# Seven outer products split a second time, with the inner instances of two products interleaved

## The chip, the cores and the metric

The kernel runs on one core of a Trainium2 chip. The metric is device time in microseconds (us), from runs of the whole program. The engines are TensorE (PE, matrix products), VectorE (DVE), ScalarE (ACT), GpSimd (POOL) and SyncE (SP). In this kernel POOL and SP mostly issue transfers (DMAs). Each engine works through its own list of instructions in order; a waiting instruction holds up all that stand behind it on that engine.

## What is computed

A soft mixture of experts: every token goes through all 8 experts, and the results are added with the softmax of the router's logits as weights.

```python
batch, seq, hidden, n_experts, expert_hidden = 16, 512, 512, 8, 2048
probs = softmax(router_logits, axis=-1)          # (16, 512, 8)
for e in range(n_experts):
    expert_out = np.matmul(x, expert_weights[e])  # (16, 512, 512) x (512, 2048)
    output += probs[:, :, e:e+1] * expert_out
```

Scaling the rows of x by the probabilities first turns this into one product of matrices, Z (8192 tokens by 8 x 512) times W (8 x 512 by 2048), with the sum over the experts inside it. The kernel works in 16-bit floats and adds up in 32 bits.

## The kernel before

The big product is cut in two along each of its three dimensions: rows into even and odd blocks of 256 tokens (one even and one odd block are a row pair, 16 of them), experts into two groups of four (2048 of the inner dimension), and columns into two halves of 1024. A scheme of the Strassen-Winograd kind turns the 8 block products into 7, which the code numbers 1 to 7 and which are called outer products here. Their left operands are sums and differences of blocks of Z, their right operands of blocks of W. One outer product of one row pair has 256 rows, 2048 inner and 1024 columns. Computed directly it takes 64 matmuls of 128x128 by 128x512.

Products 1, 5, 2 and 4 are computed by `sub_product`, one after the other over all row pairs. It splits each product once more by the same scheme, with the two row pairs of a step as the two halves of its rows: 7 inner instances, each of two row blocks of 8 matmuls (`K8 = 8`), where the direct form needs 8. Results of products 1, 2 and 5 go to memory of their own (`kept`) and those of 4 to the output. Behind them, a loop over the 16 row pairs (`for q in range(NI)`) computes products 6 and 7 directly (`plain`, 64 matmuls each), and product 3 by an inner split within the row pair (`prod`, 7 instances of 8 matmuls; for q = 0 directly). It reads back what was kept and writes the output, part of it by DMAs that add to what stands there. The first two row pairs of product 1 are computed directly at the very start, while the weights are still arriving.

Left operands are made by DVE: `mul` or `times` multiplies transposed x with probabilities (128 partitions by 2048 elements, 16 bits), and differences of such tiles follow. Right operands of the inner split are made by `inner_sums`, whose four steps (5, 6, 4, 7) each are one DVE operation over 128 by 4096. Weight tiles have 15 places (`wpool`), left tiles 10 (`zpool`), x and probability tiles 8 (`xpool`), and half tiles (128 rows by 512 columns in 32 bits, `half`) 15. PE adds up in 8 banks of PSUM of that size.

The order of the work on each engine comes from two sources. Where `pinned` holds (the start, and the loop over row pairs), DVE and ACT instructions keep the order in which the code writes them (`keep_in_program_order` in `dve`); in `sub_product` a scheduler at compile time chooses. DMAs of POOL and SP and the matmuls are placed by that scheduler throughout, with a few pinned by `behind`.

The lines that matter in the profile: line 142 is `mm`, every matmul; line 122 is `tt`, every two-operand DVE operation, to be told apart by tile names (z left tiles, w weight tiles, h half tiles, ps banks) and shapes; line 136 is POOL's loads, line 133 SP's DMAs, line 594 POOL's stores to the output, line 404 ACT's copies out of PSUM in `sub_product`, line 669 those in the loop.

Of the kernel before, what the change touches and what calls it, by code (L numbers as in the profile page):

```python
# [20 lines left out]

# [11 lines left out]
def kernel(  # L33
# [7 lines left out]
    nc = tc.nc  # L41
# [24 lines left out]
    zpool = ctx.enter_context(tc.tile_pool(name="zpool", bufs=10))  # L66
    xpool = ctx.enter_context(tc.tile_pool(name="xpool", bufs=8))
    hpool = ctx.enter_context(tc.tile_pool(name="hpool", bufs=1))
# [5 lines left out]
    used = {i: -1 for i in range(15)}  # L74
    places = {}
    turn = count()

    def share(**sizes):

        order = sorted(used, key=used.get)  # L80
        for use, n in sizes.items():
            places[use], order = [order[:n], 0], order[n:]

    def h_tile(shape, dtype, use="any"):
        mine, i = places[use]
        places[use][1] = (i + 1) % len(mine)
        used[mine[i]] = next(turn)
        return hpool.tile(shape, dtype, name="h", tag=f"h{mine[i]}")

    share(any=15)  # L90


# [3 lines left out]


# [10 lines left out]

    pinned = [True]

    def note(i):
        last[i.ins.engine] = i.ins

    def dve(i):
        note(i)
        if pinned[0]:
            tc.keep_in_program_order(i)
# [17 lines left out]
    def pool(o, i):  # L135
        note(nc.gpsimd.dma_start(out=o, in_=i))  # L136
# [4 lines left out]
    def mm(ps, z, w, start, stop):  # L141
        nc.tensor.matmul(ps, z, w, start=start, stop=stop, skip_group_check=True)  # L142


# [5 lines left out]

    def cast_w(q, kn, e, t, parts=1):
        k, n = kn
        for c in range(0, C, C // parts):
            pool(t[:, ds(e * C + c, C // parts), :],
                 expert_weights[(q // 10 - 1) * HE + 2 * k + e, ds(c * P, C * P // parts),
                                ds((q % 10 - 1) * NH + n * NB, NB)].rearrange("(c p) n -> p c n", p=P))

    def load(what, kn, gate=True):
        t = new_w()
        if gate:  # L160
            dve(nc.vector.memset(t.rearrange("p (e c) n -> p e c n", e=2)[:, :, 0, 0:2], 0.0))  # L161
        if (what, kn) in stored:
            pool(t, stored[what, kn])
        else:
            for e in range(2):
                cast_w(what, kn, e, t)
        return t

    def store(what, kn, t):
        stored[what, kn] = d = dram.tile([P, K8, NB], f16, name=f"wd{what}_{kn[0]}{kn[1]}")  # L170
        sp(d, t)

    def inner_sums(b, t3=None):

        t3 = t3 or b[0, 1]
        w = {1: b[0, 0], 2: b[1, 0], 3: b[1, 1], 7: t3}

        def step(p, x, y):
            if p not in w:
                w[p] = new_w()  # L180
            tt(w[p], x, y, SUB)
        return w, [lambda: step(5, b[0, 1], b[0, 0]), lambda: step(6, b[1, 1], w[5]),
                   lambda: step(4, w[6], b[1, 0]), lambda: step(7, b[1, 1], b[0, 1])]

    def inner_weights(b):
        w, sums = inner_sums(b)
        sums[0]()
        yield
        sums[1]()
        sums[2]()  # L190
        yield
        sums[3]()
        return w


    def softmax(lg, J, pf=None):
# [7 lines left out]
        if pf is None:  # L204
            pf = h_tile([P, E, J], f32)
# [5 lines left out]
    P2, P1, PQ = 0, HE, 2 * HE  # L211

# [25 lines left out]
    with behind():  # L238
        for kn in BLOCKS[:3]:
            for e in range(2):  # L240
                cast_w(11, kn, e, b11[kn], 2 if kn == (0, 0) and e == 0 else 1)
    cast_x(4)
    cast_x(6)
    for e in range(2):
        cast_w(11, BLOCKS[3], e, b11[BLOCKS[3]])

    def early_p(t):
        return softmax(lg0[t], 4, cpool.tile([P, HE, 4], f16, name=f"ph0_{t}"))
# [13 lines left out]

# [12 lines left out]

# [18 lines left out]

# [13 lines left out]
    def softmax_of_all():  # L308
        pf = softmax(lg_all, J)
        ph = h_tile([P, 3 * HE, J], f16)  # L310
        nc.scalar.copy(ph[:, 0:HE], pf[:, HE:E])
        nc.scalar.copy(ph[:, HE:2 * HE], pf[:, 0:HE])
        tt(ph[:, 2 * HE:], pf[:, 0:HE], pf[:, HE:E], ADD)
        for r in range(R):
            sp(p_dram[:, :, ds(r * J, J)], ph[ds(r * NHQ, NHQ)])


    x_dram = {}
    x_new = []

    def load_x(h):
        xT = xpool.tile([P, C, HQ], f16, name="xT", tag="x")
        if h in x_dram:
            sp(xT, x_dram[h])
        else:
            xs = h_tile([P, HQ // P, H], f16, "xs")
            pool(xs, x_f[ds(h * HQ, HQ), :].rearrange("(j p) h -> p j h", p=P))
            for j in range(HQ // P):
                note(nc.sync.dma_start_transpose(out=xT[:, :, ds(j * P, P)], in_=xs[:, j, :]))
            x_new.append((h, xT))  # L330
        return xT

    def store_x():
        while x_new:
            h, xT = x_new.pop()
            x_dram[h] = dram.tile([P, C, HQ], f16, name=f"x_{h}")
            sp(x_dram[h], xT)

    def load_p(h, first):
        pT = xpool.tile([P, HE, HQ], f16, name="pT", tag="x")  # L340
        sp(pT, p_dram[h, ds(first, HE), :].partition_broadcast(P))
        return pT

    def mul(xT, pT, e0, ne, t0, nt):
        z = zpool.tile([P, ne, C, nt], f16, name="z", tag="z")
        tt(z, xT[:, :, ds(t0, nt)].unsqueeze(1).to_broadcast([P, ne, C, nt]),
           pT[:, ds(e0, ne), ds(t0, nt)].unsqueeze(2).to_broadcast([P, ne, C, nt]), MUL)
        return z.rearrange("p e c t -> p (e c) t")


    kept = {r: [dram.tile([2, HQ, NB], f32, name=f"kept{r}_{i}") for i in range(NI)] for r in (1, 2, 5)}

    def half(use="any"):
        return h_tile([P, NB], f32, use)

    def out_rows(i, odd, u, cols, n):
        return out_f[ds((2 * i + odd) * HQ + u * P, P), ds(cols * NH + n * NB, NB)]

    def to_kept(r, i, u, n, t):
        if r == 4:  # L360
            sp(out_rows(i, 1, u, 0, n), t)
        else:
            sp(kept[r][i][n, ds(u * P, P), :], t)

    def from_kept(r, i, u, n, use):
        t = half(use)
        sp(t, kept[r][i][n, ds(u * P, P), :])
        return t

    def sub_product(r, odd, first, w, prep, start=0, xp=None, rest=()):  # L370

        for d in range(start, NI // 2):
            hs = [4 * d + odd, 4 * d + 2 + odd]
            xp = xp or [(load_x(h), load_p(h, first)) for h in hs]
            a11, a12 = (mul(*xp[0], e0, 2, 0, HQ) for e0 in (0, 2))
            a21, a22 = (mul(*xp[1], e0, 2, 0, HQ) for e0 in (0, 2))
            xp = None

            def new(a, b, op):
                z = zpool.tile([P, K8, HQ], f16, name="z", tag="z")  # L380
                tt(z, a, b, op)
                return z
            s1 = new(a21, a22, ADD)
            s2 = new(s1, a11, SUB)
            s4 = new(a12, s2, SUB)
            tt(a21, a11, a21, SUB)
            for make in rest:
                make()
            rest = ()
            z = {1: a11, 2: a12, 3: s4, 4: a22, 5: s1, 6: s2, 7: a21}  # L390

            for u in range(HQ // P):
                banks = {}

                def prod(p, b, start=True):
                    if start:
                        banks[b] = bank()
                    for k in range(K8):
                        mm(banks[b], z[p][:, k, ds(u * P, P)], w[p][:, k, :], start and k == 0, k == K8 - 1)
                    return banks[b]  # L400

                def keep(ps):
                    t = half("r")
                    nc.scalar.copy(t, ps)  # L404
                    return t

                def put(t, n, a, b, op):
                    o = half("o")
                    tt(o, a, b, op)
                    to_kept(r, 2 * d + t, u, n, o)  # L410

                r1 = keep(prod(1, "x"))
                put(0, 0, prod(2, "b"), r1, ADD)
                r5 = keep(prod(5, "q"))
                r2 = keep(prod(6, "x", False))
                put(0, 1, prod(3, "q", False), r2, ADD)
                prod(7, "x", False)
                r3 = keep(banks["x"])
                put(1, 1, banks["x"], r5, ADD)
                put(1, 0, r3, prod(4, "d"), SUB)  # L420
            with behind():
                store_x()
                next(prep, None)
# [349 lines left out]
```

## Time and profile before

| what | value |
|---|---|
| time, median of 3 runs | 1433.58 us (1433.33 to 1433.64) |
| span of the profiled execution, first to last instruction | 1431.8 us |
| other time given for that execution | none; the span is 1.8 us under the median |
| PE busy | 1424.9 us, 100% |
| DVE busy | 1031.8 us, 72% |
| ACT busy | 271.0 us, 19% |
| POOL busy | 220.0 us, 15% |
| matmuls at line 142 with left tiles | 6560 |
| moved by DMA | 318.92 MB, 223 GB/s on average |

How to read it. The shares are busy time over the span. A busy PE may still be slower than its peak, because matmuls overlap: each has 379 ns from its start to its end, but the next one starts long before that. The chain that ended last goes back from the last instruction to what released it, step by step, and so says which engine sets the end. A line of a group of instructions has the code line, the engine, the operation, the tiles written and read, the shapes, the count, and then the total busy time, the mean of one in nanoseconds, and the idle time ahead of these instructions with what ended it. A line of the view in order of time has the start, the duration, the engine, the line, the operation and the count of instructions merged into it; what stands in brackets is the idle time before and its releaser. Instructions of one engine can overlap a little, so the distance of two starts can be less than a duration.

### The profile page before, as it was taken

The page shows a single profiled execution, that of the slowest core. Times are in us where ns is not written, and L with a number is a line of the kernel's source. Part 1 is how long each engine was busy: PE and PEld are TensorE (multiplying, and loading weights), DVE is VectorE, ACT ScalarE, POOL GpSimd, SP SyncE. Part 2 cuts the span into 40 slices and gives each one's busy share as a digit, 9 for nine tenths or more (in the row PEclk, how much of TensorE's full clock was granted, in tenths as well). Part 3 has the DMA queues.
Part 4 walks back from the last instruction along what each step waited for, and adds up shares of the span by engine and source line. Part 5 has one row for each costly group of instructions (what it writes and reads, how often), then busy time and mean ns, then how long its engine had stood idle before and what let it go on. Part 6 is the DMA issues. An engine that isn't in the chain of part 4 may idle for free.

```text
span 1431.8 us, 18014 instructions
## 1 busy us (share of the span) xinstructions
PE 1424.9 (100%) x6654; PEld 648.0 (45%) x6654; DVE 1031.8 (72%) x1177; ACT 271.0 (19%) x472; POOL 220.0 (15%) x344
## 2 busy tenths in 40 slices
PE   9999999999999999999999999999999999999998
PEld 4444444444444444444444444444444444444444
DVE  6967585657686867766767687777777877877773
ACT  3211111111111111111111211111111111111111
POOL 3111100110001000001000222222222222222220
PEclk9999999999999999999999999999999999999999
DMA  9899967899649994367875977787877777778774
GB/s 196 182 252 267 273 160 192 183 256 262 204 148 305 350 333 155 132 186 220 219 250 179 311 218 232 235 239 230 229 231 223 206 216 215 225 234 241 215 199 103
DMA packets 192041, 318.92 MB, mean 223 GB/s; under 512 B 51664, under 2 KB 80592, under 8 KB 187344
## 3 DMA queue, kind: packets, MB, share of 16 engines
q1 hardware_dynamic: 135328, 202.92, 45.2%
q0 software_dynamic: 56624, 114.84, 34.1%
q8 instruction: 52, 0.85, 0.2%
q14 instruction: 37, 0.30, 0.1%
HBM read 180.13 MB, written 159.58 MB: 237 GB/s over the span
## 4 chain that ended last, share of the span: by engine, by line
PE 98%; DMA 1%; POOL 0%; DVE 0%; issue 0%; POOLq 0%
PE ps L142 98%; DMA w<-in_expert_weights_dram 1%; POOL w L136 0%; DVE z L122 0%; DVE h L122 0%; POOL ident L235 0%; POOLq L235 0%; POOLq L757 0%
## 5 line engine op out<-in xcount | busy, mean ns | idle before, releaser
L142 PE MATMUL ps<-w,z 128*128 128x512 f16 x6560 | 1415.2, 379 | 1.2 <-DMA w<-in_expert_weights_dram 0.9
L142 PEld LDWEIGHTS <-z 128*128 128x128 f16 x6560 | 641.6, 98 | 773.6 <-DVE z L122 1.1
L122 DVE TENSOR_TENSOR h<-ps,h 128x512 f32<-128x512 f32 x389 | 268.0, 689 | 328.5 <-PE ps L142 94.4
L122 DVE TENSOR_TENSOR z<-xT,pT 128x2048 f16<-128x2048 f16 x252 | 304.2, 1218 | 32.6 <-PE ps L142 31.2
L122 DVE TENSOR_TENSOR z<-z 128x2048 f16<-128x2048 f16 x280 | 303.6, 1108 | 7.3
L404 ACT COPY h<-ps 128x512 f32<-128x512 f32 x248 | 145.3, 586 | 602.0 <-PE ps L142 596.0
L594 POOL DMA_DIRECT2D out_dram<-h x244 | 154.1, 666 | 516.2 <-DVE h L122 305.5
L122 DVE TENSOR_TENSOR w<-w 128x4096 f16<-128x4096 f16 x36 | 82.3, 2286 | 0.4 <-DMA w<-wd 0.3
L669 ACT COPY h<-ps 128x512 f32<-128x512 f32 x64 | 37.5, 586 | 178.0 <-PE ps L142 176.3
L136 POOL DMA_DIRECT2D h<-in_x_dram x30 | 21.3, 711 | 264.0 <-DMA xT<-h 212.0
L122 DVE TENSOR_TENSOR h<-h,ps 128x512 f32<-128x512 f32 (+1 forms) x78 | 52.7, 676 | 11.1 <-PE ps L142 10.5
L136 POOL DMA_DIRECT2D w<-in_expert_weights_dram x41 | 30.7, 763 | 187.0 <-DVE w L161 130.8
L649 ACT ACTIVATE ps<-h 128x512 f32<-128x512 f32 x35 | 21.0, 601 | 147.0 <-DVE h L122 146.5
L122 DVE TENSOR_TENSOR h<-h 128x512 f32<-128x512 f32 (+1 forms) x67 | 45.9, 684 | 3.6 <-DMA h<-kept 3.5
L627 ACT COPY ps<-h 128x512 f32<-128x512 f32 x64 | 35.5, 593 | 52.5 <-DMA h<-kept 52.5
L136 POOL DMA_DIRECT2D w<-wd x12 | 6.5, 545 | 206.0 <-DVE w L161 132.7
L729 ACT COPY h<-ps 128x512 f32<-128x512 f32 x15 | 8.8, 586 | 120.7 <-PE ps L142 120.7
L718 ACT COPY h<-ps 128x512 f32<-128x512 f32 x15 | 8.8, 586 | 17.1 <-PE ps L142 17.1
L136 POOL DMA_DIRECT2D w<-wdt x8 | 4.4, 555 | 21.9 <-DVE w L161 21.9
L260 DVE CAST z<-ps 128x512 f16<-128x512 f32 x8 | 5.2, 686 | 3.5 <-PE ps L142 3.4
L260 DVE CAST xT<-ps 128x512 f16<-128x512 f32 x4 | 2.6, 686 | 5.9 <-PE ps L142 5.9
L142 PEld LDWEIGHTS <-w 128*128 128x128 f16 x80 | 5.0, 98 | 2.6 <-DMA w<-in_x_dram 0.9
(37 smaller groups left out, 44.6 us busy)
## 6 DMA issues: line engine op xcount, KB each, us to landing
out_dram<-h POOLq DMA_DIRECT2D x244, 256.0 KB, 4.8
kept<-h SPq DMA_DIRECT2D x192, 256.0 KB, 4.3
h<-kept SPq DMA_DIRECT2D x192, 256.0 KB, 4.5
pT<-p_dram SPq DMA_DIRECT2D x124, 256.0 KB, 4.9
w<-in_expert_weights_dram POOLq DMA_DIRECT2D x39, 512.0 KB, 13.1
out_dram<-h SPq DMA_DIRECT2D x75, 256.0 KB, 3.5
xT<-x SPq DMA_DIRECT2D x62, 256.0 KB, 3.1
w<-wd POOLq DMA_DIRECT2D x12, 1024.0 KB, 11.1
```

The costliest lines, as they stand in the source:

```text
L122: dve(nc.vector.tensor_tensor(out=o, in0=a, in1=b, op=op))
L136: note(nc.gpsimd.dma_start(out=o, in_=i))
L142: nc.tensor.matmul(ps, z, w, start=start, stop=stop, skip_group_check=True)
L260: dve(nc.vector.tensor_copy(o, ps))
L404: nc.scalar.copy(t, ps)
L594: queue.dma_start(out=out_rows(self.q, odd, tn[0], cols, tn[1]), in_=o, **how)
L627: act(nc.scalar.copy(x, rows.m1[tn]))
L649: act(nc.scalar.mul(banks[b], v, scale))
L669: act(nc.scalar.copy(c21, x))
L718: act(nc.scalar.copy(r1, x))
L729: act(nc.scalar.copy(r3, x))
```

## The change

All seven outer products are now split a second time within each row pair. An inner instance has 128 rows, 1024 inner and 512 columns: 8 matmuls. Seven of them (`STEPS`) make one outer product of one row pair, 56 matmuls where the direct form takes 64. The exception is product 1 of the first two row pairs, which is still done directly at the start.

The outer scheme has other signs than before, so that each product is finished with what is already there: a product starts either alone, or on a base, a half tile that is read back from memory or taken from the product before, and that its results are added to. Product 1's results are kept; 2 is added to 1; 5 writes the output; 6 is added to 1 minus 5 (`joined`); 7 is added to the output rows that 6 wrote; 4 is added to 7 and then accumulated into the output by the DMA, and 3 is accumulated into the output by the DMA.

The work is a list of 57 stages (`stages`). A stage has two products of row pairs, (r,q) and (r',q'), whose inner instances alternate (slot 0 is the first step of the first, slot 1 the first step of the second, and so on to slot 13), or one product with seven slots. The order is: three stages (1,q)(1,q+1); eight stages (2,q)(1,q+1); four stages (2,q)(2,q'); one stage (5,0)(5,1); a single stage (6,0); fourteen stages (6,q)(5,q+1); a single stage (6,15); one stage (7,0)(7,1); a single stage (4,0); fourteen stages (4,q)(7,q+1); a single stage (4,15); eight stages (3,q)(3,q+1). The seven weight tiles of both products of a stage are resident, 14 of the 15 places of `wpool`; the 15th takes a tile of a later product, and where one product gives way to the next, the other tiles are loaded into places as the slots release them (`retire`).

From the first stage on, every instruction of every engine keeps the order that the code writes (`ordered[0] = True`). DVE's preparatory work is written out from one queue of tasks, each with a nominal cost in us, by a running credit. Each slot adds `SLOT` = 1.73 to it; while it is positive, the next task is written; the operations that empty the banks after a slot (`post`) and all tasks are charged to it; it is capped at 1.73 above and has no limit below. A slot that needs a task which has not been written yet writes all tasks up to that one first (`need`). Left operands of a stage are queued after slot 0 of the stage before (`queue_lefts`): two tiles t0 and t1, and their inner difference s2; a second inner difference, i, is queued at the start of its own stage. x and probabilities are asked for two stages ahead (`start_loads`), the transposes of new x follow after slot 6 (`finish_loads`), and the bases are read one stage ahead.

The weights of the outer products are made in the early stages by `wedge`, half a block at a time: two pieces are cast from memory, and three or four DVE operations make pieces of the weights of products 7, 5, 6 and 4, which POOL writes to memory (`kept_w`) and SP reads back later (`fetch_w`). The rest of 4's weights are made later (`t4_at`).

Other edits: the places of the pools change (`zpool` 9 and 3 smaller, `xpool` 10, half tiles 12); POOL instead of SP stores the kept results; the softmax for the first tokens and for all tokens has a few more small sums, because the probabilities of odd rows are combined differently; the last instance changes its order of steps and its base.

The core of the diff:

```diff
-    zpool = ctx.enter_context(tc.tile_pool(name="zpool", bufs=10))
-    xpool = ctx.enter_context(tc.tile_pool(name="xpool", bufs=8))
-    hpool = ctx.enter_context(tc.tile_pool(name="hpool", bufs=1))
+    zpool = ctx.enter_context(tc.tile_pool(name="zpool", bufs=9))
+    spool = ctx.enter_context(tc.tile_pool(name="spool", bufs=3))
+    xpool = ctx.enter_context(tc.tile_pool(name="xpool", bufs=10))
+    hpool = ctx.enter_context(tc.tile_pool(name="hpool", bufs=12))
...
     def note(i):
         last[i.ins.engine] = i.ins
+        if ordered[0]:
+            tc.keep_in_program_order(i)
...
+    ordered[0] = True
+    SLOT = 1.73
+    STEPS = (1, 5, 6, 2, 7, 3, 4)
...
+        def run(self):
+            self.done = True
+            credit[0] -= self.cost
+            self.make()
+
+    def need(task):
+        while task is not None and not task.done:
+            queue.popleft().run()
...
+    def slack():
+        credit[0] += SLOT
+        while queue and credit[0] > 0:
+            queue.popleft().run()
+        credit[0] = min(credit[0], SLOT)
...
+        def make(self, k):
+            if self.of is not None:
+                need(self.of.task[k])
+            t = self.t[k] = new_z()
+            times(t, k, self.xb, self.pb)
+            if self.less is not None:
+                u = new_z()
+                times(u, k, *self.less)
+                tt(t, t, u, SUB)
+            if self.of is not None:
+                tt(t, self.of.t[k], t, SUB)
+
+        def queue_make(self, k):
+            cost = 1.22 + (2.33 if self.less is not None else 0) + (1.11 if self.of is not None else 0)
+            self.task[k] = later(cost, lambda: self.make(k))
...
+            self.task["s2"] = later(0.58, make)
...
+            self.task["i"] = later(1.15, make)
...
+        def queue_sum(self, sums, p):
+            self.task[p] = later(2.29, sums[p])
...
+        def step(self, p):
+            b = "q" if p in (5, 3) else "b" if p == 2 else "x"
+            if p in (1, 5):
+                self.banks[b] = bank()
+            z, w = self.left.op(p), self.right.op(p)
+            for k in range(K8):
+                mm(self.banks[b], z[:, k, :], w[:, k, :], p in (1, 5) and k == 0, k == K8 - 1)
...
+        def post_alone(self, p, x, q, b):
...
+                credit[0] -= 0.69
+                tt(o[TN[p]], x if p == 7 else q, o[TN[p]], ADD)
...
+            if p == 2:
+                act(nc.scalar.copy(o[tn], b))
+                return
+            credit[0] -= 0.69
+            if p == 1:
+                self.banks["b"] = bank()
+                tt(self.banks["b"], x, o[tn], ADD)
+            else:
+                tt(o[tn], q if p in (5, 3) else x, o[tn], ADD)
...
+    def run(stage):
+        some = stages[stage]
+        for p in some:
+            p.left.queue_i()
+        n = 0
+        for i in range(len(STEPS)):
+            for p in some:
+                for make in hooks.get((stage, n), ()):
+                    make()
+                p.step(p.steps[i])
+                slack()
+                p.post(p.steps[i])
+                n += 1
+                if n == 1:
+                    start_loads(stage + 2)
+                    queue_lefts(stage + 1)
+                if n == 5:
+                    store_loads(stage + 1)
+                if n == 7:
+                    finish_loads(stage + 2)
...
+    def retire(stage, r, of, fetch):
...
+        for slot, kn in zip((2, 4, 6), order[1:]):
+            at(stage, slot, lambda kn=kn: fetch(kn))
+        sums_at(stage, 13, r, of, (5, 6))
+        sums_at(stage + 1, 2, r, of, (7, 4))
+    retire(k7 - 2, 7, t3, lambda kn: t3.__setitem__(kn, fetch_w("t3", kn)))
...
+    sums_at(k7, 8, 4, t4, (5, 6))
+    sums_at(k7, 11, 4, t4, (7, 4))
+    retire(k4 - 1, 3, b22, lambda kn: b22.__setitem__(kn, cast_block(22, kn)))
```

## The prediction

> **What bounds the kernel now.** I read the shares of busy time first, then the chain that ended last, then the groups by shape, then VectorE (DVE) in order of time.
>
> ```profile
> span 1431.8 us, 18014 instructions
> PE 1424.9 (100%) x6654; PEld 648.0 (45%) x6654; DVE 1031.8 (72%) x1177; ACT 271.0 (19%) x472; POOL 220.0 (15%) x344
> PE 98%; DMA 1%; POOL 0%; DVE 0%; issue 0%; POOLq 0%
> L142 PE MATMUL ps<-w,z 128*128 128x512 f16 x6560 | 1415.2, 379 | 1.2 <-DMA w<-in_expert_weights_dram 0.9
> ...
> 46.10 0.78 issue
> 46.88 1.23 DVE z L122
> 48.11 0.05 issue
> 48.16 1379.81 PE ps L142 x6400
> ```
>
> TensorE (PE) carries 98% of the chain. The last four lines are its pieces in order of time: from 48.16 us to the end PE never waits. One matmul takes 1379.81 / 6400 = 0.2156 us there; with the 16 halves of the last instance counted as 8, 1415.2 / 6552 = 0.2160. I use 0.2157. One inner instance, eight matmuls, is a slot of 1.73 us.
>
> ```profile
> L122 DVE TENSOR_TENSOR z<-xT,pT 128x2048 f16<-128x2048 f16 x252 | 304.2, 1218 | 32.6 <-PE ps L142 31.2 <-issue 1.4
> L122 DVE TENSOR_TENSOR h<-ps,h 128x512 f32<-128x512 f32 x389 | 268.0, 689 | 328.5 <-PE ps L142 94.4 <-ACT h L669 73.1 <-issue 67.7
> L122 DVE TENSOR_TENSOR z<-z 128x2048 f16<-128x2048 f16 x220 | 263.6, 1222 | 6.3
> L122 DVE TENSOR_TENSOR w<-w 128x4096 f16<-128x4096 f16 x36 | 82.3, 2286 | 0.4 <-DMA w<-wd 0.3
> L122 DVE TENSOR_TENSOR z<-z 128x1024 f16<-128x1024 f16 x60 | 40.0, 688 | 1.0
> ...
> 36.80 2.35 DVE L122 TENSOR_TENSOR z<-xT,pT 128x2048 f16<-128x2048 f16 x2
> 39.07 2.29 DVE L122 TENSOR_TENSOR w<-w 128x4096 f16<-128x4096 f16 x1
> 41.27 1.22 DVE L122 TENSOR_TENSOR z<-z 128x2048 f16<-128x2048 f16 x1
> ...
> 1257.65 0.69 DVE L122 TENSOR_TENSOR h<-ps,h 128x512 f32<-128x512 f32 x1 [2.72 <-ACT h L669]
> 1258.26 1.22 DVE L122 TENSOR_TENSOR z<-xT,pT 128x2048 f16<-128x2048 f16 x1
> 1259.51 1.23 DVE L122 TENSOR_TENSOR z<-z 128x2048 f16<-128x2048 f16 x1
> ```
>
> These give DVE's prices as distances from start to start. A half tile out of PSUM: 1258.26 - 1257.65 = 0.61. A product of 2048: 1.13 when the next does not need it (two in 2.35), 1.25 when it does (1259.51 - 1258.26); I take 1.17. A weight sum: 41.27 - 39.07 = 2.20. The 128x1024 difference: 0.68 busy, taken whole. A PSUM result is ready 0.379 - 0.216 = 0.16 after its slot. DVE's result frees PE 0.06 later (48.10 to 48.16). So a post, the operation that empties a bank after a slot, ends 0.16 + 0.61 = 0.77 after the slot.
>
> **What it removes.** Products 6 and 7 took 64 matmuls for each of 16 row pairs, and 3 took 64 for the first; an inner split takes 56. That is 2 x 16 x 8 + 8 = 264 matmuls, 264 x 0.2157 = 56.9 us, all on the path.
>
> **What it adds and moves, edit by edit.** ACT's seeds and copies stay with ACT at 0.59 each. DVE now also writes a PSUM bank (bank b = x + base). No row shows that; the nearest are 0.69 (from PSUM) and, on ACT, 0.601 into PSUM against 0.586 out of it. 0.61 it is, with 0.69 as the upper end. Results written aside and read back go from 6 MB per row pair to about 3.5. POOL takes over the stores of product 1 from SP and writes 120 accumulating stores instead of 64: some 540 issues by 0.67 (its 666 ns row) are 360 us, a quarter of the span. Behind a waiting store on POOL stand later stores, casts of x and of weights; x is asked for two stages ahead. The first three stages are denser: 6.3 MB of casts, 4.2 MB of derived weights and 12 MB of x, p and stores in 72.5 us are about 310 GB/s, against the 254 GB/s at a DMA share of 1.04 that 100 to 200 us show. The 56 GB/s too much are 4 MB, 15 us at 254. I take 0, since PE never idled under that share of 1.04 before, and keep +15 as an end. New weights land in a full pool, each as a slot gives its tile back; a cast of 512 KB lands in 13.8 us there, and the sums that need them come 7 to 11 slots (12 to 19 us) later: 0, end +5.
>
> **The order that DVE is given.** This decides. After the early part every engine keeps the written order. A task (left factors t0, s2, t1, i; weight sums) is written out when the credit is above zero. The credit gains 1.73 per slot and is charged each task and post at its nominal cost (post 0.69, t0 or t1 of products 7 and 3 3.55, a sum 2.29). If a slot needs a task that still waits in the queue, all tasks up to it are written right there, behind the post of the slot before. That post waits for PE, and PE waits for the task: neither hides the other. The debt is charged, but the time that PE stood still is not credited, and debt has no floor. The credit is a count in the code, so which tasks are forced can be counted before any run.
>
> Most stages pay their way: a stage of two products gains 24.2, and pairs (1,1), (2,1), (2,2), (6,5) and (4,7) charge 11 to 21.3. The stages of one product gain 12.1. Stage (6,15) must also make the left factors of two products 7 (2 x 7.68) and sums of weights 7. Slot by slot it spends 4.1 on posts and 8.3 on tasks and starts at -0.9: it ends at -1.2 with six tasks waiting. Then, in (7,0)(7,1), numbering slots from 0:
> - slot 1 needs t0 of the second product: 0.77 + t1 3.51 (taken in slot 0) + post 0.61 + t0 3.51 + 0.06 - slot 1.73 = 6.73
> - slot 5, s2: 0.77 + 0.68 + 0.06 = 1.51
> - slot 7, t1, with slot 6 beside it (its post is ACT's): 0.77 + 3.51 + 0.06 - 1.73 = 2.61
> - slot 8, two sums and i: 2 x 2.20 + 1.17 - 1.73 = 3.84
> - slot 9, i of the second: 0.77 + 1.17 + 0.06 = 2.00
>
> That is 16.7 us; the credit ends at -1.2 + 24.2 - 8.3 - 18.1 = -3.4, and nothing for (4,0) has been made. Single stage (4,0): t0 2.00; s2, t1 and a sum 0.77 + 4.05 + 0.06 = 4.88; a sum 3.03; two sums and i, over one slot, 4.67: 14.6 us, credit -8.7. Every later (4,q)(7,q+1) gains 24.2, charges 8.3 + 13.0, and so pays back only 2.9. Until the debt is gone it is forced at slots 0, 1, 5, 7 and 9: 2.00 + (0.77 + 0.68 + 1.17 + 3.51 + 0.06 = 6.19) + 1.51 + 2.61 + 2.00 = 14.3. Three stages pay that, the fourth 11.3, the fifth 0.9. The same hole before product 3 is shallower, since (3,3) has only four posts: 3.7 in (4,15), then 7.0, 5.8, 2.2. Singles (6,0) and (6,15) wait 2.2 each for late posts. Sum: 2.2 + 2.2 + 16.7 + 14.6 + 42.9 + 11.3 + 0.9 + 3.7 + 7.0 + 5.8 + 2.2 = 109.5. Bounds: products of 2048 at 1.13, other operations at their shortest and no latency give about 97; 1.25 and full busy times about 125. The start keeps its wait of 2 us for DVE, the end its tail.
>
> **Sum** against the profiled execution: 1431.8 - 56.9 + 109.5 = 1484.4. The page gives no other time of this execution; the median of the runs, 1433.58, is 1.8 above its span. With that, 1486.
>
> **A rule against the change.** The row first: the granted clock is 1.00 in every stretch of this trace, and since 48 us PE had no gap. The Trainium skill, "TensorE: Matmul & The Clock Gate", section "Why this matters for your kernels", says that PE gaps above some 3 us put the clock back to half. By it, ten or so of my stalls exceed 3 us, and half a 3.4 us window lost at each would be an estimated 17 us more, 1503. No run here shows such a gap; the sum above leaves it out.
>
> **Rivals.**
> 1. DVE catches up (other side). All of DVE's work is smaller than the span: about 21 of 24.2 us in a (4,7) stage, 30 in each of the two single stages that feed 7 and 3, of which some 8 may come late. If PE waited only for what DVE cannot do in time, the stalls would be 4 for (6,0), 15 around (6,15) and (4,0), 9 around (4,15): 28 us, and 1433.6 - 57 + 28 = 1405. For it: DVE was 72% busy and PE never waited. Against it: the old order let sub-products float, the new one pins them and forces late. It decides where stalls stay under 57 us, that is, where the debt is repaid within about two stages.
> 2. DMA is the bound early. The 15 us above come on top: 1501. For: share 1.04. Against: that cost nothing before.
> 3. The change doesn't cut PE's work: 264 fewer matmuls follow from the loop bounds, and slots could only lengthen if each switch between two products cost PE; the old kernel switches banks every eight matmuls without a gap. It would give 1433.6 + 109.5 = 1543.
>
> **How the numbers follow.** Forced order as counted 0.70 (1474 to 1502 by the bounds; with other small waits to 1510), with early DMA waits on top 0.11, DVE catching up 0.16, no less PE work 0.03. The likeliest gives 1486. The range 1435 to 1530 reaches below the first for stalls half as long and above for 2 and long gaps; it leaves out most of rival 1 and all of 3. Below 0.2% (2.9 us), about what a measurement of this kernel can tell, I put 0.02; faster 0.15, slower 0.83. The likeliest one's own range is 1470 to 1512.
>
> **What would show it.** The matmul group has 6296 entries. PE is idle about 110 us, nearly all waiting for DVE on z and w tiles, in a block from about 800 to 1045 us (48 us, 30 stages of two products by 24.2 and one of 12.1 before it) and a smaller one at about 1265 to 1375, where product 3 starts; the other stages run without gaps. DVE's busy share falls in that block. Wrong would be: gaps spread evenly, gaps that end on a DMA, or a block that ends within two stages.

## The result and the profile after

The changed kernel takes 1534.19 us (median of 4 runs) against 1433.51 us: 1.071 times as long, 95% interval 1.069 to 1.073. The forecast was 1486 us, 1435 to 1530: the direction was right, but the loss is 101 us, where the forecast had 52.

The profile page of the changed kernel, its head, the chain that ended last and the four groups to compare:

```profile
span 1530.4 us, 17248 instructions
...
PE 1406.5 (92%) x6390; PEld 627.5 (41%) x6390; DVE 1109.0 (72%) x1252; ACT 181.2 (12%) x314; POOL 349.9 (23%) x547
...
PEclk9998999999999999999998789899999999999999
...
PE 70%; issue 13%; DVE 10%; DMA 4%; POOL 3%; ACT 0%; POOLq 0%; DVEq 0%; ACTq 0%
...
L127 PE MATMUL ps<-w,z 128*128 128x512 f16 x5416 | 1212.5, 385 | 104.4 <-DVE z L107 82.4
...
L107 DVE TENSOR_TENSOR h<-ps,h 128x512 f32<-128x512 f32 x418 | 283.7, 688 | 328.1 <-PE ps L127 318.9
...
L107 DVE TENSOR_TENSOR z<-xT,pT 128x2048 f16<-128x2048 f16 x284 | 339.3, 1218 | 10.1 <-DMA wdt<-z 6.2
L127 PE MATMUL ps<-w,d 128*128 128x512 f16 x880 | 201.8, 381 | 13.2 <-DVE d L107 6.9
```

The matmuls with left tiles (z and d) are 5416 + 880 = 6296, 264 fewer, as counted. The durations of DVE's operations have hardly moved: 688 and 1218 ns, where they were 689 and 1218. DVE is busy for 77 us more in all, 72% of the span as before. What changed is that PE waits. The view of waits, with PE as the waiting engine (columns: who waits for whom, total us, times, longest):

```profile
PE ps L127 <- DVE z L107: 82.4, 27, 6.7
PE ps L127 <- DVE h L107: 17.1, 5, 10.6
PE ps L127 <- DVE w L107: 7.8, 2, 4.8
PE ps L127 <- DVE d L107: 6.9, 5, 1.4
PE ps L127 <- DVE ps L107: 3.3, 2, 1.9
```

These are 117.5 us, all of them waits for DVE, 41 in number. The busy time by stretches shows where (columns: PE, PEld, DVE, ACT and POOL busy with their counts, PE's granted clock, DMA share, GB/s):

```profile
41.60:123.20 81.60, 69.40 (x321) 31.30 (x320) 55.20 (x52) 17.94 (x32) 24.56 (x40) 0.96 1.13 269
123.20:445.00 321.80, 321.76 (x1484) 145.58 (x1484) 228.82 (x255) 39.70 (x68) 87.16 (x152) 0.99 0.86 247
445.00:800.00 355.00, 351.80 (x1630) 159.30 (x1628) 276.74 (x328) 49.66 (x85) 77.70 (x137) 1.00 0.75 227
800.00:1058.00 258.00, 175.00 (x664) 68.99 (x663) 141.78 (x154) 7.04 (x12) 32.13 (x47) 0.85 0.42 114
1058.00:1300.00 242.00, 241.40 (x1119) 109.49 (x1120) 203.03 (x239) 11.73 (x20) 63.12 (x88) 1.00 0.82 198
1300.00:1384.00 84.00, 65.53 (x286) 28.28 (x285) 64.30 (x62) 12.81 (x22) 17.89 (x21) 0.94 0.69 137
```

From 800 to 1058 us PE idles for 83 us. DVE is busy for only 142 of the 258 us there (55%), less than the 84% it has from 1058 to 1300 us, with the same kind of stages and hardly a gap. So DVE is not full in the block; that it gets its work too late is what experiments 1 and 2 test. The granted clock, 0.99 to 1.00 in the stretches that have hardly a gap, is 0.85 there. One stage, (4,1)(7,2), in order of time on PE (start, duration, what, count, and in brackets the idle time before):

```profile
892.09 1.90 PE L127 MATMUL ps<-w,z 128*128 128x512 f16 x8 [1.92 <-DVE z L107]
900.11 7.60 PE L127 MATMUL ps<-w,z 128*128 128x512 f16 x24 [6.12 <-DVE z L107]
907.54 1.89 PE L127 MATMUL ps<-w,d 128*128 128x512 f16 x8
910.82 1.90 PE L127 MATMUL ps<-w,d 128*128 128x512 f16 x8 [1.38 <-DVE d L107]
912.55 1.89 PE L127 MATMUL ps<-w,z 128*128 128x512 f16 x8
917.03 5.31 PE L127 MATMUL ps<-w,z 128*128 128x512 f16 x16 [2.59 <-DVE z L107]
924.26 8.81 PE L127 MATMUL ps<-w,z 128*128 128x512 f16 x40 [1.92 <-DVE z L107]
934.99 1.90 PE L127 MATMUL ps<-w,z 128*128 128x512 f16 x8 [1.92 <-DVE z L107]
```

The DVE operations of the changed kernel between its first two slots, in the same view (the first line is the post of slot 0, which waits for PE; the three after it are the forced tasks behind it):

```profile
894.10 0.70 DVE L107 TENSOR_TENSOR ps<-ps,h 128x512 f32<-128x512 f32 x1 [2.06 <-PE ps L127]
894.71 0.68 DVE L107 TENSOR_TENSOR d<-z 128x1024 f16<-128x1024 f16 x1
895.30 3.49 DVE L107 TENSOR_TENSOR z<-xT,pT 128x2048 f16<-128x2048 f16 x3
898.83 1.22 DVE L107 TENSOR_TENSOR z<-z 128x2048 f16<-128x2048 f16 x1
903.74 0.70 DVE L107 TENSOR_TENSOR ps<-ps,h 128x512 f32<-128x512 f32 x1 [3.69 <-PE ps L127]
```

Slot 0's results are there at 894.0. PE then waits 6.12 us while DVE makes s2 and t1 of the first product and the whole t0 of the second (894.71 to 900.05); after that DVE waits 3.69 us for PE. The gaps of the stage, 1.92 (in front of slot 0), 6.12, 1.38, 2.59 and 1.92, are the five that the prediction named (2.00, 6.19, 1.51, 2.61, 2.00). New is the length of the slots after the gaps: 24 matmuls take 24 x 0.2157 + 0.16 = 5.34 us at full clock and took 7.60; 16 after the gap of 2.59 took 5.31 instead of 3.61. Two stretches at half clock account for both (columns as in the table by stretches above):

```profile
897.86:904.68 6.82, 4.57 (x11) 1.65 (x12) 2.85 (x3) 0.00 (x0) 0.00 (x0) 0.50 0.81 226
918.34:921.75 3.41, 3.41 (x10) 1.21 (x9) 0.00 (x0) 0.59 (x1) 0.57 (x1) 0.50 0.77 186
```

Half of PE's busy time in them, 2.3 and 1.7 us, is what the slots are longer. But the same gap is not always paid for. Two stages later, in (4,3)(7,4), the 16 matmuls run at full clock:

```profile
1002.11 3.63 PE L127 MATMUL ps<-w,z 128*128 128x512 f16 x16 [2.59 <-DVE z L107]
```

The two spans differ by 98.6 us. PE's idle time went from 1431.8 - 1424.9 = 6.9 to 1530.4 - 1406.5 = 123.9 us: +117.0. PE's busy time should have fallen by 56.9 to 1368.0 and is 1406.5: +38.5. -56.9 + 117.0 + 38.5 = 98.6. The 38.5 are not all slower clock. Ahead of each wait the last matmul shows its full 0.379 us, of which the next one otherwise covers 0.16: 41 x 0.16 = 6.6 us. That leaves 31.9 us for the clock. The granted clock agrees: it stands at 0.50 in 14 stretches of 3.4 to 13.7 us while matmuls are still to come, PE is busy for 63.7 us of them, and half of that is 31.9.

### The profile page after: what moved, and what is told of

It reads as the page before. It is cut to its first block, busy times and chain, and to the rows that moved or that the text cites. A ratio compares the mean times of both kernels' runs of the same rounds, so it can differ in the third digit from the quotient of the medians.

```text
span 1530.4 us, 17248 instructions
## 1 busy us (share of the span) xinstructions
PE 1406.5 (92%) x6390; PEld 627.5 (41%) x6390; DVE 1109.0 (72%) x1252; ACT 181.2 (12%) x314; POOL 349.9 (23%) x547
## 4 chain that ended last, share of the span: by engine, by line
PE 70%; issue 13%; DVE 10%; DMA 4%; POOL 3%; ACT 0%; POOLq 0%; DVEq 0%; ACTq 0%
PE ps L127 70%; DVE z L107 6%; POOL out_dram L121 2%; DMA w<-in_expert_weights_dram 2%; DVE h L107 2%; DVE w L107 1%; DMA kept<-h 1%; DMA wdt<-z 1%; DVE d L107 1%; POOL xs L121 0%; DMA h<-out_dram 0%; DMA out_dram<-h 0%; POOL w L121 0%; DMA h<-kept 0%; DVE ps L107 0%
## 5 line engine op out<-in xcount | busy, mean ns | idle before, releaser
L127 PE MATMUL ps<-w,z 128*128 128x512 f16 x5416 | 1212.5, 385 | 104.4 <-DVE z L107 82.4
L127 PEld LDWEIGHTS <-z 128*128 128x128 f16 x5416 | 534.7, 99 | 771.3 <-DVE z L107 96.5
L121 POOL DMA_DIRECT2D out_dram<-h x376 | 243.8, 674 | 975.3 <-ACT h L524 478.3
L107 DVE TENSOR_TENSOR z<-xT,pT 128x2048 f16<-128x2048 f16 x284 | 339.3, 1218 | 10.1 <-DMA wdt<-z 6.2
L127 PE MATMUL ps<-w,d 128*128 128x512 f16 x880 | 201.8, 381 | 13.2 <-DVE d L107 6.9
L127 PEld LDWEIGHTS <-d 128*128 128x128 f16 x880 | 86.1, 98 | 120.1 <-DVE d L107 9.4
L107 DVE TENSOR_TENSOR z<-z,d 128x2048 f16<-128x2048 f16 x110 | 130.2, 1218 | 0.6 <-DMA wdt<-z 0.6
L107 DVE TENSOR_TENSOR z<-z 128x2048 f16<-128x2048 f16 x96 | 117.6, 1225 | 3.3
L524 ACT COPY h<-ps 128x512 f32<-128x512 f32 x65 | 38.1, 586 | 616.5 <-PE ps L127 615.3
L513 ACT COPY h<-ps 128x512 f32<-128x512 f32 x88 | 51.6, 587 | 382.8 <-PE ps L127 352.6
L107 DVE TENSOR_TENSOR w<-w 128x4096 f16<-128x4096 f16 (+1 forms) x47 | 90.0, 1925 | 0.7
L107 DVE TENSOR_TENSOR d<-z 128x1024 f16<-128x1024 f16 x110 | 75.6, 688 | 8.5 <-PE ps L127 6.3
L510 ACT COPY h<-ps 128x512 f32<-128x512 f32 x88 | 51.6, 586 | 175.1 <-PE ps L127 168.3
L107 DVE TENSOR_TENSOR z<-w 128x2048 f16<-128x2048 f16 x10 | 12.2, 1219 | 13.2 <-DMA wdt<-z 10.1
```

The source lines that it names most:

```text
L107: dve(nc.vector.tensor_tensor(out=o, in0=a, in1=b, op=op))
L121: note(nc.gpsimd.dma_start(out=o, in_=i, **how))
L127: note(nc.tensor.matmul(ps, z, w, start=start, stop=stop, skip_group_check=True))
L510: act(nc.scalar.copy(o[tn], q if p == 5 else x))
L513: act(nc.scalar.copy(o[TN[p]], b if p == 2 else x))
L524: act(nc.scalar.copy(o[tn], b))
```

## The experiments

All start from the changed kernel, 7 to 10 with the edits of 6 in it. The theory: a shortage of DVE time in the single stages starts a debt, the debt keeps forcing tasks behind posts that wait for PE, and PE's gaps then lower its clock. The first rival: DVE's capacity is the bound in those stages. Separate from this are two early gaps, of 1.6 us at 87 and 10.6 us at 113 us, where DVE itself waits for transfers. Its wait ahead of the second:

```profile
116.83 1.22 DVE L107 TENSOR_TENSOR z<-w 128x2048 f16<-128x2048 f16 x1 [10.14 <-DMA wdt<-z]
```

**1. No debt.**

```diff
     def need(task):
+        kept_credit = credit[0]
         while task is not None and not task.done:
             queue.popleft().run()
+        credit[0] = kept_credit
```

> One line: a forced task no longer changes the credit (the credit is put back after `need`). DVE's work, the matmuls and the DMAs stay the same; only the order in which DVE gets its tasks changes. Theory (the debt keeps the forced order alive for stages after the shortage): the count gives PE 36 us of waiting for DVE instead of 109, stages (4,2)(7,3) to (4,4)(7,5) run without gaps, and with fewer long gaps the slow-clock part falls from 38 to some 12: about 1534 - 73 - 26 = 1435 us. Rival (DVE's capacity is the bound in the stages of products 4 and 7): the block from 800 to 1058 us keeps its length and the time stays near 1530.

Measured: 1439.09 us, 1.0043 times before (1.0030 to 1.0057). The same stretch in two parts, by busy time (columns as above):

```profile
800.00:900.00 100.00, 78.66 (x323) 33.03 (x322) 78.59 (x81) 3.52 (x6) 13.66 (x21) 0.90 0.53 161
900.00:1058.00 158.00, 158.00 (x734) 71.62 (x732) 139.72 (x166) 7.62 (x13) 36.25 (x52) 1.00 0.75 196
```

PE's waits in this kernel:

```profile
PE ps L127 <- DVE z L107: 25.6, 7, 6.7
PE ps L127 <- DVE h L107: 17.4, 5, 11.1
PE ps L127 <- DVE ps L107: 4.0, 3, 1.9
```

From 900 to 1058 us PE has no gap, with the same work on the same engines; DVE is at 88%. Without the two early gaps, 1.5 and 11.1 us here, the waits are 34.4 us (36 expected). PE's busy time is 1381.0 - 1368.0 = 13.0 us above that of the full clock; without the 0.16 at each of 15 waits, 10.6 us are the slow clock (12 expected). The rival falls: two added lines, which change neither an operation nor a transfer, are worth 95 us.

**2. Forced tasks three slots earlier, debt as it was.**

```diff
+    LOOK = 3
...
+    def ahead(stage, n):
+        coming = slots(stage) + (slots(stage + 1) if stage + 1 < len(stages) else [])
+        for p, s in coming[n + 1:n + 1 + LOOK]:
+            for t in (p.left.task.get(KEY[s]), p.right.task.get(s)):
+                if t is not None and not t.done and t in queue:
+                    need(t)
...
                 p.step(p.steps[i])
+                ahead(stage, n)
                 slack()
```

> Forced tasks are written three slots ahead of their slot, ahead of the post, with the debt charged as in the changed kernel. If a forced task costs because it stands behind the post that waits for PE (theory), it now runs beside the slots: by the count PE waits 38 us for DVE instead of 109, with the gaps at slots 5, 7 and 9 gone and the one at slot 1 of (4,q)(7,q+1) down from 6.1 to about 1: about 1437 us. If the debt itself, and not the place behind the post, makes the gaps, the four stages after (4,0) keep their 14 us each and the time stays above 1500.

Measured: 1441.9 us (1.0058, 1.0035 to 1.0082). PE in order of time in the stretch of the debt:

```profile
895.60 5.35 PE L127 MATMUL ps<-w,z 128*128 128x512 f16 x24 [0.87 <-DVE z L107]
900.79 3.62 PE L127 MATMUL ps<-w,d 128*128 128x512 f16 x16
904.25 15.70 PE L127 MATMUL ps<-w,z 128*128 128x512 f16 x72
920.83 5.35 PE L127 MATMUL ps<-w,z 128*128 128x512 f16 x24 [0.88 <-DVE z L107]
```

One gap of 0.87 us is left of 14 us per stage, though tasks are forced there as before. PE's waits add up to 48.0 us, 13.1 of them early; the other 34.9 answer to the 38 expected. So a debt by itself costs next to nothing; it costs because a forced task was written behind the post of the slot just before. Both edits take away the gaps of these stages, so their gains can't be added up; no run has the two together.

**3. Earlier left factors, debt and forcing as they were.**

```diff
-                p.left.queue_make(0)
-                p.left.queue_s2()
-                p.left.queue_make(1)
+                if not p.left.task:
+                    p.left.queue_make(0)
+                    p.left.queue_s2()
+                    p.left.queue_make(1)
...
+    def one_left(p):
+        p.left.queue_make(0)
+        p.left.queue_s2()
+        p.left.queue_make(1)
+    at(k7 - 2, 8, lambda: one_left(products[7, 0]))
+    at(k4 - 1, 8, lambda: one_left(products[3, 0]))
```

> The left factors of the first product of (7,0)(7,1) and of (3,0)(3,1) are queued one stage earlier, after slot 7 of the last stage of two products ahead of the single one, where DVE has time to spare. Credit and debt stay as in the changed kernel. Theory (the shortage in the single stages starts the debt, and the debt does the rest): before product 3 the shortage is gone and with it all gaps after (4,15) but some 1 us (18.7 us before); before product 7 it is smaller, the debt begins one stage later and is gone after (4,2)(7,3) instead of (4,4)(7,5), 46 us of gaps instead of 86. By the count PE waits 49 us in all, slow clock some 16 us: 1534 - 60 - 22 = 1452 us. If the shortage is not where the debt begins, the blocks keep their lengths and the time stays above 1500.

Measured: 1458.2 us (1.0175, 1.0155 to 1.0195). PE's waits add up to 60.5 us, 11.2 of them in the two early gaps; the other 49.3 answer to the 49 expected. Behind (4,15) no gap is left; in it one of 4.1 us stands where there were 1.3 and 2.2. The gaps of products 7 and 4 end at 951 us instead of 1058. The shortage in the single stages is where the debt begins.

**4. PE kept busy in its long gaps.** 186 added matmuls give results that nobody uses.

```diff
             z, w = self.left.op(p), self.right.op(p)
+            for k in range(self.fill.get(p, 0)):
+                mm(self.banks[b], ones, self.moving[:, k % K8, :], True, True)
...
+                p.moving = some[0].right.w[1]
                 p.step(p.steps[i])
...
+    for (r, q, p), n in {(7, 1, 1): 28, (4, 0, 5): 18, (7, 2, 1): 26, (7, 3, 1): 26, (7, 4, 1): 26,
+                         (7, 5, 1): 18, (3, 1, 1): 20, (3, 3, 1): 24}.items():
+        products[r, q].fill[p] = n
```

> PE gets 186 matmuls more that nobody uses, in the eight longest gaps (slot 1 of the stages that wait for a left factor, 18 to 28 each), into a bank that the next real matmul starts afresh; their operands are already there. Theory (a long gap lowers PE's clock after it, and that is the 38 us that the slots of these blocks are longer): the waits for DVE end at the same moments, the granted clock in 800 to 1058 us rises from 0.85 to 0.92 or more, and about half of the 38 us go: 1515 us. Rival (the slots are long for another reason, or the clock falls for the sum of all gaps): 1534 us or more.

Measured: 1517.26 us, 17 us less than the changed kernel with 186 matmuls more. A filled gap on PE, in order of time:

```profile
886.81 5.78 PE L127 MATMUL ps<-w,ones 128*128 128x512 f16 x26
893.09 5.35 PE L127 MATMUL ps<-w,z 128*128 128x512 f16 x24 [0.51 <-DVE z L107]
```

The busy time of the stretch, and its granted clock:

```profile
800.00:1058.00 258.00, 204.14 (x886) 85.92 (x884) 158.60 (x173) 8.20 (x14) 34.97 (x51) 0.97 0.48 128
```

The 24 matmuls after the filled gap take 5.35 us, where they took 7.60, and the granted clock is 0.97 instead of 0.85. PE's busy time beyond that of the full clock: 1432.0 - 186 x 0.2157 - 1368.0 = 23.9 us instead of 38.5, with as many waits as before, so the slow clock went from 31.9 to 17.3 us. Filling the long gaps takes away the slow stretches behind them. The rest stands behind gaps that were not filled, the early one among them; of the four gaps of 2.6 us ahead of 16 matmuls two cost nothing here (3.63 us) and two 1.6 and 1.7 us (5.20 and 5.31).

**5. The early gaps: another queue for the temporary pieces.**

```diff
-            send("t3", u)
+            sp(kept_w("t3", kn)[:, rows, :], u)
...
-            send("t4", u)
+            sp(kept_w("t4", kn)[:, rows, :], u)
```

> The early weight pieces in temporary left tiles (of products 7 and 4) are stored by SP instead of POOL; nothing else changes. Theory: the two early gaps (1.6 us at 87 and 10.6 us at 113) come from stores that stand behind the casts on POOL's queue, so that the next DVE piece waits 6.2 and 10.1 us for a left tile; through SP they land in some 4 us, the gaps fall to 2 us or less, and the time is 1534 - 10 = 1524 us. Rival (the DMA engines as a whole are full, whatever the queue): the gaps stay, 1534 us.

Measured: 1526.54 us (1.0648, 1.0617 to 1.0679), 8 us better. The two gaps are 2.1 and 3.6 us instead of 1.6 and 10.6. By itself this looked like POOL's queue.

**6. The three together:** experiments 1, 3 and 5.

> Earlier factors, no debt, and the stores of the temporary pieces by SP together. By the count PE waits for DVE 11 us instead of 109, none over 2.5 us, so that hardly any slow clock is left (2 us), and the early gaps keep the 6 us and 2 us of slow clock that the run with SP stores showed: 1433.5 - 56.9 + 13 + 8 = 1398 us, faster than before by 2.5%. If the three causes share their time (rival), the sum falls short and the time is above 1415.

Measured: 1404.12 us, 0.9794 of before (0.9778 to 0.9811): the fewer matmuls now show. From its page:

```profile
span 1403.4 us, 17231 instructions
...
PE 1374.5 (98%) x6390; PEld 622.9 (44%) x6390; DVE 1105.2 (79%) x1252; ACT 181.1 (13%) x314; POOL 345.1 (25%) x537
```

PE's waits:

```profile
PE ps L127 <- DVE h L107: 12.5, 3, 9.7
PE ps L127 <- DVE z L107: 9.5, 5, 4.0
```

Of 22.2 us of waits (0.2 more stand in a smaller line) 9.7 are one early gap, which is back at 111 us in spite of SP's stores; the 12.5 others answer to the 11 expected, though one of them, in (4,15), is 4.0 us where none was to be over 2.5. The profiled execution, 1405.12 us, is 7.5 us over the forecast: some 3.7 for the early gap (6 expected), 1.5 for the other waits, and 2.5 because PE's busy time is 1374.5 - 1368.0 = 6.5 us above that of the full clock (4 expected).

**7. SP stores all early pieces.** Experiment 6, and `send` through SP:

```diff
-            pool(kept_w(what, kn)[:, rows, :], u)
+            sp(kept_w(what, kn)[:, rows, :], u)
```

> As the kernel with all three, but SP stores all early weight pieces, also those of products 5 and 6. If what is left of the early gaps (2.1 and 3.6 us with SP storing half of the pieces) is POOL's queue, they go and it is some 6 us faster than that kernel; if the DMA engines as a whole are full there, or SP's own loads of x now wait behind the stores, it is no faster or slower.

Measured: 1401.78 us (0.9781, 0.9762 to 0.9801), not to be told from experiment 6. The gap is 7.7 us.

**8. SP stores the kept results of the first three stages too.**

```diff
-                pool(kept_rows(q)(tn), o)
+                (sp if q < 8 else pool)(kept_rows(q)(tn), o)
```

> The kernel with all three edits and SP storing all early pieces, in which the gap at 111 us is 7.7 us; now SP also stores the kept results of the first three stages (6.3 MB), as it did before the change. The bytes are the same, POOL's queue has a third less. If the gap comes from the order on POOL's queue, it falls below 3 us and the time by 5 us or more, to 1396 us; if the 16 DMA engines as a whole are full in that stretch, the gap stays at 6 us or more and the time within 2 us of 1402, or it is slower because loads of x stand behind stores that wait.

Measured: 1408.5 us, a gap of 14.2 us. A shorter queue on POOL doesn't help. This doesn't clear the queues altogether, since SP's grew: from 42 to 120 us the transposes of x that SP issues took 12.1 us to land (median), where they took 9.8 in experiment 7.

**9. Two casts later.** On experiment 7:

```diff
-    at(1, 6, lambda: cast21((1, 1)))
-    at(1, 12, lambda: cast21((1, 0)))
+    at(2, 0, lambda: cast21((1, 1)))
+    at(2, 4, lambda: cast21((1, 0)))
...
-    sums_at(2, 5, 2, b21, (5, 6))
-    sums_at(2, 10, 2, b21, (7, 4))
+    sums_at(2, 8, 2, b21, (5,))
+    sums_at(2, 13, 2, b21, (6,))
+    sums_at(3, 2, 2, b21, (7, 4))
```

> The same kernel; the casts of two of the four weight blocks of product 2 come 18 and 14 slots later (slots 0 and 4 of the third stage), and the sums that need them 3 to 6 slots later. POOL still stores the kept results. Some 1 MB less is cast (2 MB less is read) before the gap at 111 us. If the engines as a whole are full, the gap goes (below 2 us) and a gap of up to 5 us may open where the sums now wait for the later casts: 1396 us, at worst 1402. If it is the order on POOL's queue behind other casts, the gap stays near 7.7 us.

Measured: 1402.34 us, a gap of 7.6 us: nothing gained.

**10. And four DVE pieces later.** On experiment 9:

```diff
-    wedge_at(1, 2, (0, 1), 1, (1, 3))
+    wedge_at(1, 2, (0, 1), 1, (1, 9))
```

> The kernel with later casts; in addition the four DVE pieces of the second half of the first weight block are queued six slots later in the third stage (slot 9 instead of 3). In the kernel with later casts DVE waits 9.3 us for x at 95 us and 3.6 us for a left tile at 111 us, and the posts that PE needs stand behind these pieces. Theory (the late transfers alone would be covered; the pieces written ahead of the posts uncover them): the gap of 7.6 us at 111 us falls below 2 us, and the time by 6 to 9 us with the slow clock after it, to some 1395 us. Rival (whatever DVE does there, data are late by that much): a gap of 5 us or more stays in the third or fourth stage and the time is within 2 us of 1402.

Measured: 1406.24 us (0.9806, 0.9789 to 0.9822). PE's gap in order of time:

```profile
129.57 6.20 PE L127 MATMUL ps<-w,d 128*128 128x512 f16 x16 [7.21 <-DVE ps L107]
```

DVE's waits for transfers ahead of it, in the same view:

```profile
104.08 1.22 DVE L107 TENSOR_TENSOR z<-xT,pT 128x2048 f16<-128x2048 f16 x1 [6.77 <-DMA xT<-xs]
...
126.55 2.36 DVE L107 TENSOR_TENSOR z<-z,d 128x2048 f16<-128x2048 f16 x2 [7.85 <-DMA wdt<-z]
```

The gap moved six slots on, as far as the pieces, and is as long. Neither queue, place nor the time of two casts removes it. Whether the DMA engines as a whole are full there is not shown. Their share is 1.11 to 1.14 from 42 to 120 us in the changed kernel and in all ten experiments; but the kernel before has 1.15 from 111 to 135 us without a gap. Experiment 9 was to make the gap go if the engines are full, and it stayed; yet from 42 to 120 us that kernel still moved 264 GB/s, where experiment 7 moved 265, so no run took bytes away. The cause of the early gaps stays open. They are 12 of the 101 us.

## Why the prediction was right or wrong

- **What it removes** was right: 264 matmuls fewer, and 56.9 us that came out once the waits were gone.
- **The order that DVE is given** was right in mechanism, place and size: single gaps agree to some 0.15 us where nothing else moves (slot 1 of (7,0)(7,1): 6.73 counted, 6.71 shown idle and 0.16 for the end of the matmul ahead of it, which the count includes). PE's waits for DVE are 117.5 us; without the early 12.2 they are 105.3, and with 0.16 for each of these 39 waits 111.5, where the sum had 109.5. The block was expected from 800 to 1045 us and stands from 800 to 1058.
- **Rival 1, DVE catches up,** was rightly put below: it does so only when the order is changed (experiments 1 and 2). That its figure of 1405 us is close to what the repaired kernels reach is in part luck: of its 28 us of waits experiment 6 has 12.5, and an early gap of 9.7 and 6.5 us of longer busy time make up the rest.
- **The step that failed: the clock was left out of the sum.** The sum put the slower clock after PE's gaps at nothing; the range allowed for an estimated 17 us, from one half-clock window after each of some ten gaps above 3 us. It measured 31.9, the largest single miss. There were ten such gaps, as estimated, but the half-clock stretches behind them, up to 13.7 us long, cost 22.3 us. Four more stretches stand behind gaps of 1.9 to 2.9 us, which the estimate didn't count, and cost 9.5: in (4,1)(7,2) the gap of 6.12 cost 2.3 us, and the gap of 2.59 us that opened 14 us later another 1.7. The Trainium skill's "TensorE: Matmul & The Clock Gate", section "Why this matters for your kernels", warns of gaps above some 3 us. The trace agrees that gaps of that size lower the clock (0.85 in the block), and shows a loss after some gaps of 2.59 as well. The reason I gave for leaving it out, that no run so far showed such a gap, says only that the old trace couldn't price it. A sum that forecasts gaps of 5 and 6 us should have carried the term.
- **Early DMA waits** were taken at 0 with an end of 15 us; they were 12.2. The bytes per stage that I had worked out, a fifth above what the old trace had moved, spoke for the end and not for 0. PE's untouched run under a share of 1.04 before was no evidence for a heavier load. Rival 2, which put them on top, was right that the time is lost there; its reason, that DMA is the bound, stays open.
- Both terms point the same way. The end of the range held both at their estimated sizes, 1486 + 17 + 15 = 1518; the clock was nearly twice its estimate, and so the time came out above 1530. With all terms as measured, the early waits with their two ends of 0.16, 1484.4 + 31.9 + 12.5 + 2.0 = 1530.8, against a span of 1530.4 us.

## What to carry to other kernels

Where the order of work is written out by a budget, count what the budget does after a shortage: here a debt that was charged for work done while the bottleneck engine stood still kept forcing work late for stages after the shortage was over. Work that a step needs should be written ahead of the last operation that waits for that engine, not behind it; three slots of look-ahead or two lines of bookkeeping were each worth over 90 us here; the bookkeeping with two smaller edits beside it turned a loss of 7% into a gain of 2%. And when a forecast holds gaps on TensorE of a few microseconds, price the slower clock after them too.

## What I had not expected of the hardware

The slow stretches after gaps cost 31.9 us for 117 us of gaps. Useless matmuls in the gaps made the kernel 17 us faster, with 186 instructions more on its busiest engine. The response to short gaps isn't uniform: in the changed kernel the same gap of 2.59 us, ahead of the same 16 matmuls, cost 1.7 us in three stages, (4,1)(7,2), (4,2)(7,3) and (4,4)(7,5), and nothing in the one between, (4,3)(7,4). No run shows what decides it.
